# First norm's factor moved from the input to the products, its gain load moved to the end: one core of a layer with attention, scan and experts

## The chip, the cores and the metric

One NeuronCore of a Trainium2 chip runs the program. The metric is the device time of one execution in microseconds, the median of several runs. The kernel before takes 455.46 us (three runs, 455.26 to 455.54).

## What is computed

256 tokens of 1024 channels go through one layer: a norm, a projection of 5632 columns, two mixers (stick-breaking attention and a gated recurrence in chunks), gates, an output projection, a second norm, a router that gives each token 2 of 16 experts, the experts, and a last norm. What matters here is the first line of the mixer:

```python
def rmsnorm(x, g):
    var = jnp.mean(xf * xf, axis=-1, keepdims=True)
    return xf * lax.rsqrt(var + EPS) * g

h = rmsnorm(x, ln1_g)
proj = h @ w_in
```

The factor rsqrt(var + EPS) is one number for each token; g is one number for each channel. The factor can therefore be put on h or, token by token, on proj.

## The kernel before

TensorE multiplies in fp32r, and each operand is split in a high and a low part (h and l in the names): three products stand for one (hh, hl, lh). ScalarE makes the high part by a copy, VectorE or GpSimd the low part by a subtraction (`split`).

**Start.** `x2` holds x as two tiles of 128 tokens, loaded by two transfers on SyncE's queue. TensorE runs small matmuls on the identity (`warm`), and the row of gains `ln1_g` is transposed to a column `g1c`. For each of the two token tiles ScalarE squares x with a running sum, `rms_scale` forms the factor (Ln and Exp on ScalarE, one Newton step on VectorE), and VectorE multiplies x by it (`xn`). TensorE transposes `xn` in sixteen 128x128 blocks into four PSUM banks (`pts`, tags B0, B1, C0, C1), and from there ScalarE writes `hTH` and VectorE `hTL`, channel block by channel block, times `g1c`.

**Projection.** `COLS` and `WIDE` list the order of the weight columns: ten chunks of 256 columns (`half`), then six of 512 columns in two halves each (`wide`). `pre(n)` loads the weights of chunk n into a ring of three buffers, 1 MB each, and splits them. A chunk of the first ten is 48 products of 128x128 by 128x256 into one PSUM bank (tags A0 and A1 in turn), with the columns on the partitions and the tokens along the row. Chunk 0 runs its three parts one behind the other (L315); the others run hh, hl, lh for each channel block (`mm3`, L202 to L204). Behind each chunk comes its eviction: `ev_f` for chunks 0 and 1 (sigmoid, then the decay), `ev_q` for 2 and 3 (silu, then a product with kS on GpSimd), `ev_g` for 4 and 5, plain copies (qkT) for 6 to 9. `tasks` hangs the mixers' own pieces behind chunks: `vectors` (transposes of small constants) behind the first half of chunk 0, `diag` (the matmuls `pd` on GpSimd's product, then `dg` and `at`) behind chunk 4, the seven `level`s of the recurrence from chunk 5 on. A level needs masks (`lmask`) that GpSimd makes at the start.

**Order.** TensorE's instructions run as they are written. For the other engines a scheduler sets the order; `tc.issue_after(i)` puts instructions of the same engine behind i, `nosync` adds such an edge by hand.

**Experts.** Eight pairs of experts: for each, gate, up and down weights of 12 MB go through a ring of twenty buffers that the earlier stages leave (the list `state["tags"]`, tL the last of them), all on SyncE's queue, in the order of `load_gu` and `load_d`. TensorE runs the gate products, the up products, the scatter of the pair before (`py`), transposes, and the down products. `load_gain` loads `final_g`, spread over 128 partitions (0.5 MB), into tL; it stands in the last pair between the gate and the up weights:

```python
    def load_gu(p):
        for nm, w in (("g", w_gate), ("u", w_up)):
            if p == NP - 1 and nm == "u":
                load_gain()
```

Of the kernel before, what the change touches and what calls it, by code (L numbers as in the profile page):

```python
# [9 lines left out]
F32 = mybir.dt.float32  # L10
F32R = mybir.dt.float32r
# [7 lines left out]
P = 128  # L19
# [11 lines left out]
def hybrid_kernel(ctx: ExitStack, tc: tile.TileContext, x, ln1_g, w_in, w_bsb, w_bhg, hg_norm_g,  # L31
# [43 lines left out]
    act_set(EXPLN)  # L75
# [6 lines left out]
    nc.scalar.dma_start(rowa, ln1_g.rearrange("(k p) -> k p", p=P))  # L82
    nc.scalar.dma_start(rows[0:8], hg_lb.rearrange("r (k p) -> (r k) p", p=P))
# [33 lines left out]
    nc.gpsimd.memset(lmask, 1.0)  # L117
    for i, B in enumerate(LV):
        mv = lmask[:, i].rearrange("p (n b) -> p n b", b=B)
        n = 64 // B  # L120
        nc.gpsimd.affine_select(mv, mv, [[-2 * B, n], [0, B]], ALU.is_ge, 0.0, base=0,
                                channel_multiplier=1)
        nc.gpsimd.affine_select(mv, mv, [[2 * B, n], [0, B]], ALU.is_ge, 0.0, base=B - 1,
                                channel_multiplier=-1)
# [20 lines left out]
    warm(8, "A1")  # L145
# [7 lines left out]
    warm(5, "A1")  # L153

    def rms_scale(dst, ss, n, nm):
# [4 lines left out]
        nc.vector.tensor_scalar(v, ss, -0.5 / n, -0.5 * EPS, ALU.mult, ALU.add)  # L160
        act(y, y, AF.Exp, scale=-0.5)
# [20 lines left out]
    def split(raw, shape, k, pieces=1, pool=()):  # L182
# [4 lines left out]
        for i in range(pieces):  # L187
            sl = slice(i * n, i * n + n)
            if pieces == 4 and i >= 2:
                nc.vector.tensor_copy(h[:, sl], raw[:, sl])  # L190
            else:
                marks["split"] = act(h[:, sl], raw[:, sl], AF.Copy).ins
            low = (nc.gpsimd if i in pool else nc.vector).tensor_sub(l[:, sl], raw[:, sl], h[:, sl].bitcast(F32))  # L193
# [21 lines left out]
    def pre(n):  # L215
# [4 lines left out]
        elif n < NCH:  # L220
            c = COLS[n]
            raw = load(wv[:, :, c * 256:(c + 1) * 256], [KT, 256])
            chunks[n] = split(raw, [KT, 256], "p%d" % c, **({"pieces": 4, "pool": (0, 1, 3)} if n == 0 else {"pieces": 2}))
# [6 lines left out]
    marks["xn"] = marks["g1c"]  # L230
    for t in range(2):
        with tc.issue_after(marks["xn"]):
            act(xn[:, t], x2[:, t], AF.Square, accum_out=ss1[:, t:t + 1])
            rms_scale(ss1[:, t:t + 1], ss1[:, t:t + 1], D, "n1%d" % t)
            marks["xn"] = nc.vector.tensor_scalar_mul(xn[:, t], x2[:, t], ss1[:, t:t + 1]).ins
    with tc.issue_after(marks["xn"]):
        pre(0)
    pts = [ps.tile([P, 2, NTOK], F32, name="pt%d" % k2, tag=["B0", "B1", "C0", "C1"][k2]) for k2 in range(4)]
    for t in range(2):
        for k in range(KT):  # L240
            nc.tensor.transpose(pts[k // 2][:, k % 2, t * P:(t + 1) * P], xn[:, t, k * P:(k + 1) * P], ident)
    for k2 in range(4):
        for k in (2 * k2, 2 * k2 + 1):
            marks["hT"] = act(hTH[:, k], pts[k2][:, k % 2], AF.Copy, scale=g1c[:, k:k + 1]).ins
        for k in (2 * k2, 2 * k2 + 1):
            marks["hL"] = nc.vector.scalar_tensor_tensor(hTL[:, k], pts[k2][:, k % 2], g1c[:, k:k + 1],
                                                         hTH[:, k].bitcast(F32), ALU.mult, ALU.subtract).ins
# [973 lines left out]
```

## Time and profile before

| | us |
|---|---|
| median of 3 runs | 455.46 (455.26 to 455.54) |
| the profiled execution | 457.36 |
| its span, first to last instruction | 455.6 |
| TensorE busy in the span | 434.5 (95%) |
| VectorE, ScalarE, GpSimd busy | 194.3, 150.1, 102.1 |
| mean granted TensorE clock | 0.986 |
| share of TensorE in the chain that ended last | 87% |

The span lies within the execution's time; what is around it is the difference. The chain follows the last instruction back, at each step to what released it. The granted clock is a share of 2.4 GHz. Times in the rows are microseconds from the span's start unless they say ns. L12 is a line of the kernel; L60 is the helper of every ScalarE operation. PE is TensorE, PEld its weight loads, DVE VectorE, ACT ScalarE, POOL GpSimd, SP SyncE; a q behind the name is the engine's queue. Adjacent TensorE instructions overlap in the timeline, since their ends are modelled: prices are taken from a group's length by its count.

### The profile page before, as it was taken

The page shows a single profiled execution, that of the slowest core. Times are in us where ns is not written, and L with a number is a line of the kernel's source. Part 1 is how long each engine was busy: PE and PEld are TensorE (multiplying, and loading weights), DVE is VectorE, ACT ScalarE, POOL GpSimd, SP SyncE. Part 2 cuts the span into 40 slices and gives each one's busy share as a digit, 9 for nine tenths or more (in the row PEclk, how much of TensorE's full clock was granted, in tenths as well). Part 3 has the DMA queues.
Part 4 walks back from the last instruction along what each step waited for, and adds up shares of the span by engine and source line. Part 5 has one row for each costly group of instructions (what it writes and reads, how often), then busy time and mean ns, then how long its engine had stood idle before and what let it go on. Part 6 is the DMA issues. An engine that isn't in the chain of part 4 may idle for free.

```text
span 455.6 us, 6088 instructions
## 1 busy us (share of the span) xinstructions
PE 434.5 (95%) x2429; PEld 285.5 (63%) x2429; DVE 194.3 (43%) x317; ACT 150.1 (33%) x244; POOL 102.1 (22%) x119
## 2 busy tenths in 40 slices
PE   6999999999999999999999999999999999999980
PEld 5999999987887888887754336343543436343340
DVE  4959875775744845794651202121120202111032
ACT  4654326354656855362430101101020101101122
POOL 7434943877142400081200000000000000000000
PEclk8899999999999999999999999999999999999997
DMA  8755444236867899739769999999999999976942
GB/s 286 238 179 182 135 117 162 93 96 190 292 238 270 309 325 411 278 132 372 292 227 414 388 426 421 421 421 423 421 420 424 418 421 423 420 313 229 401 155 99
DMA packets 38702, 135.31 MB, mean 297 GB/s; under 512 B 2366, under 2 KB 14714, under 8 KB 26892
## 3 DMA queue, kind: packets, MB, share of 16 engines
q1 hardware_dynamic: 38480, 134.75, 77.1%
q8 instruction: 21, 0.34, 0.3%
q0 software_dynamic: 128, 0.09, 0.2%
q14 instruction: 13, 0.11, 0.1%
q10 hardware_dynamic: 60, 0.02, 0.0%
HBM read 133.80 MB, written 1.05 MB: 296 GB/s over the span
## 4 chain that ended last, share of the span: by engine, by line
PE 87%; POOL 4%; DVE 3%; issue 2%; ACT 1%; DMA 1%; SPq 0%; POOLq 0%; ACTq 0%; DVEq 0%
PE pu L995 12%; PE pg L995 12%; PE pd L1024 10%; PE pv L300 5%; PE pv L302 5%; PE pv L301 5%; PE py L1040 4%; PE pp L202 3%; PE pp L204 3%; PE pp L203 3%; PE pg L966 3%; PE pl L371 2%; PE pd L1014 2%; PE pp L315 1%; PE pb L608 1%
## 5 line engine op out<-in xcount | busy, mean ns | idle before, releaser
L193 DVE TENSOR_TENSOR lp<-wt,hp 128x1024 fp32r<-128x1024 f32 (+1 forms) x43 | 59.5, 1403 | 24.1 <-ACT hp L60 24.1
L60 ACT ACTIVATE hp<-wt 128x1024 fp32r<-128x1024 f32 (+1 forms) x44 | 44.6, 1035 | 41.6 <-PE pp L203 26.7
L995 PE MATMUL pu<-wt,xg 128*64 128x512 f32 x256 | 57.3, 593 | 0.0
L995 PE MATMUL pg<-wt,xg 128*64 128x512 f32 x256 | 56.3, 592 | 0.0
L1024 PE MATMUL pd<-wt,mf 128*64 128x512 f32 x224 | 50.4, 598 | 0.9 <-DVE mf L1005 0.7
L721 POOL TENSOR_SCALAR rb<-ss,rb 128x1 f32<-128x1 f32 x1 | 0.5, 523 | 223.3 <-ACT junk L60 223.3
L1001 DVE SCALAR_TENSOR_TENSOR mf<-pu,cwall,mf 128x512 f32<-128x512 f32 x8 | 6.0, 752 | 93.8 <-PE pu L995 93.8
L995 PEld LDWEIGHTS pu<-wt,xg 128*64 128x64 f32 x256 | 18.5, 137 | 37.0 <-issue 35.6
L202 PE MATMUL pp<-hTH,hp 128*128 128x256 f32 x144 | 41.4, 287 | 0.0
L995 PEld LDWEIGHTS pg<-wt,xg 128*64 128x64 f32 x256 | 18.3, 137 | 36.0 <-issue 35.1
L203 PE MATMUL pp<-hTL,hp 128*128 128x256 f32 x144 | 40.7, 283 | 0.0
L204 PE MATMUL pp<-hTH,lp 128*128 128x256 f32 x144 | 40.7, 283 | 0.0
L300 PE MATMUL pv<-hp,hTH 128*128 128x512 f32 x96 | 39.7, 414 | 0.0
L301 PE MATMUL pv<-lp,hTH 128*128 128x512 f32 x96 | 37.5, 391 | 0.0
L302 PE MATMUL pv<-hp,hTL 128*128 128x512 f32 x96 | 37.5, 391 | 0.0
L1024 PEld LDWEIGHTS pd<-wt,mf 128*64 128x64 f32 x224 | 14.8, 136 | 31.7 <-issue 24.0
L1031 DVE SCALAR_TENSOR_TENSOR yh<-pd,cwall,yh 128x512 fp32r<-128x512 f32 (+1 forms) x16 | 11.7, 734 | 50.8 <-ACT yh L60 50.5
L60 ACT ACTIVATE yh<-pd,cwall 128x512 fp32r<-128x512 f32 (+1 forms) x16 | 10.8, 675 | 53.5 <-PE pd L1024 38.8
L202 PEld LDWEIGHTS pp<-hTH,hp 128*128 128x128 f32 x144 | 27.6, 191 | 0.1
L203 PEld LDWEIGHTS pp<-hTL,hp 128*128 128x128 f32 x144 | 27.6, 192 | 0.0
L204 PEld LDWEIGHTS pp<-hTH,lp 128*128 128x128 f32 x144 | 27.6, 192 | 0.0
L300 PEld LDWEIGHTS pv<-hp,hTH 128*128 128x128 f32 x96 | 18.0, 188 | 5.0 <-issue 0.8
(279 smaller groups left out, 727.5 us busy)
## 6 DMA issues: line engine op xcount, KB each, us to landing
wt<-in_w_exp_gate_dram SPq DMA_DIRECT2D x32, 1024.0 KB, 15.7
wt<-in_w_exp_up_dram SPq DMA_DIRECT2D x32, 1024.0 KB, 10.7
wt<-in_w_exp_down_dram SPq DMA_DIRECT2D x28, 1024.0 KB, 13.9
wt<-in_w_in_dram SPq DMA_DIRECT2D x22, 1024.0 KB, 5.1
wt<-in_w_out_dram SPq DMA_DIRECT2D x4, 1024.0 KB, 5.0
wt<-in_w_branch_sb_dram SPq DMA_DIRECT2D x2, 1024.0 KB
wt<-in_w_branch_hg_dram SPq DMA_DIRECT2D x2, 1024.0 KB
wt<-in_w_exp_down_dram SPq DMA_DIRECT2D x4, 512.0 KB, 12.9
```

The lines of the kernel that those rows point to most:

```text
L60: i = nc.scalar.activation(out_, in_, func, **kw)
L193: low = (nc.gpsimd if i in pool else nc.vector).tensor_sub(l[:, sl], raw[:, sl], h[:, sl].bitcast(F32))
L202: nc.tensor.matmul(dst, ah, bh, start=i == 0, stop=False)
L203: nc.tensor.matmul(dst, ah, bl, start=False, stop=False)
L204: nc.tensor.matmul(dst, al, bh, start=False, stop=i == n - 1)
L300: nc.tensor.matmul(pp, hh, wh[:, k], start=kh == k == 0, stop=False)
L301: nc.tensor.matmul(pp, hh, wl[:, k], start=False, stop=False)
L302: nc.tensor.matmul(pp, hl, wh[:, k], start=False, stop=kh == 1 and k == 3)
L966: nc.tensor.matmul(pg[:, j], xx[:, t, k * P:k * P + P], Sr[:, t * 256:t * 256 + 256], start=i == 0, stop=i == 3)
L995: nc.tensor.matmul(pt[j * 64:j * 64 + 64], xg[:, k, j * 64:j * 64 + 64], wts[nm, p, j, k // 4][:, k % 4], start=k == 0, stop=k == KT - 1)
L1024: nc.tensor.matmul(pds[c][j * 64:j * 64 + 64], aT_[:, f, j * 64:j * 64 + 64], wts["d", p, j, f // 2][:, f % 2, 512 * c:512 * c + 512], sta ...
L1040: nc.tensor.matmul(total(t, c0, c1), STa[:, p % 2, t * P:t * P + P], yh[:, hl, c0:c1], start=False, stop=False, skip_group_check=True)
```

## The change

- x is loaded by column halves of both token tiles instead of by token tiles. The transfer of `ln1_g` is issued ahead of ScalarE's table load.
- TensorE transposes x itself, right behind seven warm-up matmuls instead of thirteen; `hTH` and `hTL` are formed without the factor.
- Chunk 0's weights come in four transfers and are split in quarters by an order written out by hand (`first`), and its products run in an order of 24 steps (`todo`). Chunk 1's weights come in two transfers, and its products run by halves of the channels.
- The squares are summed in halves, two on ScalarE, two on VectorE, the later ones behind chunk 0's splits. `factors` forms both tiles' factors at once and puts each, times -1, on the diagonal of a 128x128 matrix; `spread` multiplies these by a matrix of -1 in the middle of chunk 1, which gives the factor of every token on all partitions (`fac`).
- Each of the first ten chunks is multiplied by `fac` at its eviction; the wide chunks, whose tokens lie on the partitions, take the factor as a scale. `ev_f` of chunk 0 moves behind the first half of chunk 1.
- The sums of chunks 2 and 3 go to banks B0 and B1.
- `level_masks` on GpSimd moves behind chunk 0's splits.
- `load_gain` moves behind the last pair's down weights, to buffer tH; a rarely run branch takes tL for it.

```diff
-    for t in range(2):
-        nc.sync.dma_start(x2[:, t], xv[:, t])
+    for c0 in (0, 512):
+        nc.sync.dma_start(x2[:, :, c0:c0 + 512], xv[:, :, c0:c0 + 512])
...
-    warm(8, "A1")
+    warm(5, "A1")
...
+    def x_tr(k):
+        for t in range(2):
+            nc.tensor.transpose(pts[k // 2][:, k % 2, t * P:(t + 1) * P], x2[:, t, k * P:(k + 1) * P], ident)
...
-    warm(5, "A1")
+    warm(2, "A1")
+    for k in range(KT):
+        x_tr(k)
...
+        prev["dve"] = marks["g1c"]
+        sq(0, 0)
+        sq(1, 0)
+        for k in range(6):
+            gh(k)
+            if k < 2:
+                gl(k)
+            if k == 0:
+                wh(0)
+            if k == 4:
+                wh(1)
+        wl(0)
+        wl(1)
+        wh(2)
+        gh(6)
+        gh(7)
+        wh(3)
+        for k in range(2, KT):
+            gl(k)
+        marks["low"] = wl(3)
+        wl(2)
+        sq(0, 512)
+        sq(1, 512)
...
+            nc.vector.tensor_add(ss1, ssp[:, 0], ssp[:, 1])
+            for t in range(2):
+                rms_scale(ss1[:, t:t + 1], ss1[:, t:t + 1], D, "n1%d" % t)
+            for t in range(2):
+                marks["dg"] = nc.vector.tensor_scalar(xn[:, 0, t * P:t * P + P], ident, ss1[:, t:t + 1], -1.0,
+                                                      ALU.mult, ALU.mult).ins
...
+        for t in range(2):
+            nc.tensor.matmul(pf[:, t * P:t * P + P], negone, xn[:, 0, t * P:t * P + P], start=True, stop=True)
+        nc.vector.tensor_copy(fac, pf)
...
+            todo = [(0, 0), (0, 1), (1, 0), (1, 1), (0, 2), (0, 3), (1, 2), (1, 3), (2, 0), (2, 1), (0, 4), (0, 5),
+                    (1, 4), (1, 5), (2, 2), (2, 3), (0, 6), (0, 7), (1, 6), (1, 7), (2, 6), (2, 7), (2, 4), (2, 5)]
...
-        act(qs[:, sl], pp, AF.Sigmoid)
-        nc.vector.tensor_mul(qs[:, sl], qs[:, sl], pp)
+        nc.vector.tensor_mul(qk0[:, sl], pp, facb)
+        act(qs[:, sl], qk0[:, sl], AF.Sigmoid)
+        nc.vector.tensor_mul(qs[:, sl], qs[:, sl], qk0[:, sl])
...
-                        act(qkT[:, 1, sl], pp, AF.Copy)
+                        nc.vector.tensor_mul(qkT[:, 1, sl], pp, facb)
...
-            if p == NP - 1 and nm == "u":
-                load_gain()
...
-        gf["g"] = blk("tL", [2, D], name="gfin")
+        gf["g"] = blk("tH", [2, D], name="gfin")
...
         load_d(p)
+        if p == NP - 1:
+            load_gain()
```

In `first`, `gh(k)` and `gl(k)` are hTH and hTL of channel block k, `wh(i)` and `wl(i)` the high and low quarter i of the weights (`wh(0)` on VectorE, the others on ScalarE; `wl(2)` on VectorE, the others on GpSimd), and `sq(t, c0)` half the squares of token tile t (t = 1 on VectorE). In `todo` the first number is the part (hh, hl, lh), the second the channel block; each step is two products.

TensorE before, from the program's start to the second chunk (pt are the transposes, pp the products, hp and lp the weights' high and low part):

```order
L142 MATMUL warm_124<-ident 128x128 x8
L151 MATMUL pcol<-ident,rowt 128x8
L142 MATMUL warm_138<-ident 128x128 x5
L241 MATMUL pt_178<-ident,xn 128x128 x2
...
L241 MATMUL pt_181<-ident,xn 128x128 x2
L315 MATMUL pp_238<-hTH,hp_168 128x256 x16
L315 MATMUL pp_238<-hTL,hp_168 128x256 x16
L315 MATMUL pp_238<-hTH,lp_169 128x256 x16
L272 MATMUL pcol_287<-ident,rowt 128x20
```

And in the changed kernel (hfirst and lfirst are chunk 0's weights):

```order
L144 MATMUL warm_109<-ident 128x128 x5
L158 MATMUL pcol<-ident,rowt 128x8
L144 MATMUL warm_124<-ident 128x128 x2
L152 MATMUL pt_115<-ident,x_66 128x128 x4
...
L152 MATMUL pt_118<-ident,x_66 128x128 x4
L402 MATMUL pp_240<-hTH,hfirst 128x256 x4
L402 MATMUL pp_240<-hTL,hfirst 128x256 x4
...
L402 MATMUL pp_240<-hTH,lfirst 128x256 x8
L356 MATMUL pcol_289<-ident,rowt 128x20
```

The transposes read x_66, the loaded x, in place of xn, stand behind two warm-ups, and the products alternate between their parts.

VectorE before, from the eviction of chunk 2 to the diagonal (L332 is the second half of a silu, lp are splits, dg reads the diagonal's matmuls):

```order
L193 TENSOR_TENSOR lp_436<-wt_433,hp_435 128x1024
L332 TENSOR_TENSOR qs<-qs,pp_379 128x512
L193 TENSOR_TENSOR lp_436<-wt_433,hp_435 128x1024
L336 TENSOR_TENSOR QZ<-qs,kf 64x2x256 x2
L193 TENSOR_TENSOR lp_498<-wt_495,hp_497 128x1024
L332 TENSOR_TENSOR qs<-qs,pp_441 128x512
L193 TENSOR_TENSOR lp_498<-wt_495,hp_497 128x1024
L336 TENSOR_TENSOR QZ<-qs,kf 64x2x256 x2
L358 COPY dg<-pd 128x16
```

And in the changed kernel (cst holds fac; esg and qs take the products times the factor):

```order
L425 TENSOR_TENSOR esg<-pp_387,cst 128x512
L199 TENSOR_TENSOR lp_445<-wt_442,hp_444 128x1024
L427 TENSOR_TENSOR qs<-qs,esg 128x512
L199 TENSOR_TENSOR lp_445<-wt_442,hp_444 128x1024
L431 TENSOR_TENSOR QZ<-qs,kf 64x2x256 x2
L425 TENSOR_TENSOR esg<-pp_450,cst 128x512
L199 TENSOR_TENSOR lp_508<-wt_505,hp_507 128x1024
L427 TENSOR_TENSOR qs<-qs,esg 128x512
L199 TENSOR_TENSOR lp_508<-wt_505,hp_507 128x1024
L431 TENSOR_TENSOR QZ<-qs,kf 64x2x256 x2
L436 TENSOR_TENSOR qs<-pp_513,cst 128x512
L455 COPY dg<-pd 128x16
```

One pass more stands ahead of each chunk's first split, and one of chunk 4 (L436) ahead of dg.

SyncE's queue before, in the last pair:

```order
L177 DMA wt_3045<-in_w_exp_gate_dram 128x2048
L1047 DMA gfin<-in_final_g_dram 128x1024
L177 DMA wt_3049<-in_w_exp_up_dram 128x2048
```

And in the changed kernel:

```order
L1036 DMA wt_3074<-in_w_exp_down_dram 128x2x256
L1146 DMA gfin<-in_final_g_dram 128x1024
L1202 DMA out_dram<-sq 128x512
```

The gain's transfer has moved past four up loads and twelve down loads to the place ahead of the outputs.

## Rows read from the trace of the kernel before

**Rows 1.** Busy time by stretch: length, each engine's busy us, clock, DMA share, GB/s.
```profile
0.00:21.70 21.70, 17.30 (x102) 16.32 (x103) 14.64 (x35) 12.27 (x23) 14.29 (x35) 0.84 0.79 256
21.70:39.60 17.90, 17.90 (x151) 17.90 (x151) 12.21 (x24) 8.29 (x11) 7.18 (x7) 1.00 0.59 189
```

**Rows 2.** The same table by single microseconds, around the first chunk.
```profile
8.00:9.00 1.00, 0.00 (x0) 0.00 (x0) 0.96 (x3) 0.00 (x0) 0.00 (x0) 0.99 0.94 299
9.00:10.00 1.00, 0.94 (x5) 0.94 (x6) 0.82 (x5) 0.95 (x2) 0.23 (x1) 0.50 1.09 359
...
15.00:16.00 1.00, 1.00 (x7) 1.00 (x7) 1.00 (x4) 1.00 (x3) 1.00 (x2) 0.59 0.00 0
```

**Rows 3.** Chain of waits up to chunk 1: start, length, what ran.
```profile
1.26 4.77 DMA x<-in_x_dram
...
9.73 1.87 DVE xn L235
11.64 1.97 PE pt L241 x8
13.62 6.76 PE pp L315 x48
...
21.01 0.31 PE pp L202
```

**Rows 4.** Timeline, first 21 us: start, length, instruction, count, [idle before <- releaser].
```profile
1.75 3.78 PE L142 MATMUL warm<-ident 128*128 128x128 f32 x16 [1.75 <-POOL ident masks.py:199]
...
4.75 1.06 ACT L60 ACTIVATE xn<-x 128x1024 f32<-128x1024 f32 x1 [2.66 <-DMA x<-in_x_dram]
...
5.65 1.38 PE L142 MATMUL warm<-ident 128*128 128x128 f32 x10
...
9.05 1.15 ACT L60 ACTIVATE hp<-wt 128x512 fp32r<-128x512 f32 x2 [1.25 <-DMA wt<-in_w_in_dram]
...
11.51 0.86 DVE L190 CAST hp<-wt 128x512 fp32r<-128x512 f32 x2
...
12.07 3.13 POOL L193 TENSOR_TENSOR lp<-wt,hp 128x512 fp32r<-128x512 f32 x2
12.30 1.76 DVE L193 TENSOR_TENSOR lp<-wt,hp 128x512 fp32r<-128x512 f32 x1
12.37 3.03 ACT L60 ACTIVATE hTH<-pt,g1c 128x256 fp32r<-128x256 f32 x8 [2.17 <-PE pt L241]
13.27 3.28 PE L315 MATMUL pp<-hTH,hp 128*128 128x256 f32 x16
13.98 3.21 DVE L246 SCALAR_TENSOR_TENSOR hTL<-pt,g1c,hTH 128x256 fp32r<-128x256 f32 x8
...
16.38 2.08 PE L315 MATMUL pp<-hTL,hp 128*128 128x256 f32 x16
```

**Rows 5.** VectorE's group of the same form; then the timeline around the diagonal.
```profile
L332 DVE TENSOR_TENSOR qs<-qs,pp 128x512 f32<-128x512 f32 x2 | 1.4, 681 | 0.0
...
41.38 2.21 POOL L333 TENSOR_TENSOR esg<-qs,kf 128x512 f32<-128x512 f32 x1 [3.50 <-DVE qs L332]
...
44.07 1.84 PE L357 MATMUL pd<-cst,esg 128*128 128x2 f32 x16
...
57.45 2.08 PE L371 MATMUL pl<-QZ,kf 128*128 128x128 f32 x16 [1.00 <-POOL QZ L387]
```

**Rows 6.** The end: SyncE's longest single wait, busy time, timeline.
```profile
SPq L1047 <- PE pd L1024: 20.7, 1, 20.7
...
408.00:413.00 5.00, 4.83 (x28) 2.16 (x28) 1.09 (x4) 0.38 (x1) 0.00 (x0) 1.00 0.03 11
...
413.21 0.33 SPq L1047 DMA_DIRECT2D gfin<-in_final_g_dram  x1
...
416.45 7.04 PE L995 MATMUL pg<-wt,xg 128*64 128x512 f32 x32
...
423.32 8.03 PE L995 MATMUL pu<-wt,xg 128*64 128x512 f32 x32
```

More of the change, by code (lines that the diff above doesn't have):

```diff
@@ L159, in rms_scale @@
         act(y, ss, AF.Ln, bias=epst, scale=1.0 / n)
-        nc.vector.tensor_scalar(v, ss, -0.5 / n, -0.5 * EPS, ALU.mult, ALU.add)
-        act(y, y, AF.Exp, scale=-0.5)
+        marks["half"] = nc.vector.tensor_scalar(v, ss, -0.5 / n, -0.5 * EPS, ALU.mult, ALU.add).ins
+        marks["exp"] = act(y, y, AF.Exp, scale=-0.5).ins
         nc.vector.tensor_scalar(v, y, y, v, ALU.mult, ALU.mult)
@@ L188, in split @@
             sl = slice(i * n, i * n + n)
[L189 to L192, printed above, removed]
+            marks["split"] = act(h[:, sl], raw[:, sl], AF.Copy).ins
             low = (nc.gpsimd if i in pool else nc.vector).tensor_sub(l[:, sl], raw[:, sl], h[:, sl].bitcast(F32))
@@ L221, in pre @@
             c = COLS[n]
-            raw = load(wv[:, :, c * 256:(c + 1) * 256], [KT, 256])
-            chunks[n] = split(raw, [KT, 256], "p%d" % c, **({"pieces": 4, "pool": (0, 1, 3)} if n == 0 else {"pieces": 2}))
+            raw = load(wv[:, :, c * 256:(c + 1) * 256], [KT, 256], parts=2 if n == 1 else 1)
+            for k in (0, 4) if n == 1 else ():
+                nc.sync.dma_start(raw[:, k:k + 4], wv[:, k:k + 4, c * 256:(c + 1) * 256])
+            chunks[n] = split(raw, [KT, 256], "p%d" % c, pieces=2)
     hTH = blk("tH", [KT, NTOK], F32R, "hTH")
@@ L239, in hybrid_kernel @@
[L239 to L247, printed above, removed]
+    ssp = cp.tile([P, 2, 2], F32, name="ssp")
@@ new lines, in hybrid_kernel, with first, then, gh @@
+    fac = cst[:, 1344:1600]
+    def first():
+        raw = load(None, [KT, 256], parts=4)
+        c = COLS[0] * 256
+        h = blk("sh1", [KT, 256], F32R, name="hfirst")
+        l = blk("sl1", [KT, 256], F32R, name="lfirst")
+        for i in range(4):
+            nc.sync.dma_start(raw[:, 2 * i:2 * i + 2], wv[:, 2 * i:2 * i + 2, c:c + 256])
+        prev = {}
+        def then(key, i):
+            if key in prev:
+                nosync(i.ins, prev[key])
+            prev[key] = i.ins
+            return i.ins
+        def gh(k):
+            marks["hT"] = then("act", act(hTH[:, k], pts[k // 2][:, k % 2], AF.Copy, scale=g1c[:, k:k + 1]))
+        def gl(k):
+            marks["hL"] = then("dve", nc.vector.scalar_tensor_tensor(
+                hTL[:, k], pts[k // 2][:, k % 2], g1c[:, k:k + 1], hTH[:, k].bitcast(F32), ALU.mult, ALU.subtract))
+        def wh(i):
+            sl = slice(2 * i, 2 * i + 2)
+            if i < 1:
+                then("dve", nc.vector.tensor_copy(h[:, sl], raw[:, sl]))
+            else:
+                marks["split"] = then("act", act(h[:, sl], raw[:, sl], AF.Copy))
+        def wl(i):
+            sl = slice(2 * i, 2 * i + 2)
+            eng, key = (nc.vector, "dve") if i == 2 else (nc.gpsimd, "pool")
+            return then(key, eng.tensor_sub(l[:, sl], raw[:, sl], h[:, sl].bitcast(F32)))
+        def sq(t, c0):
+            y, s = x2[:, t, c0:c0 + 512], ssp[:, c0 // 512, t:t + 1]
+            if t:
+                then("dve", nc.vector.scalar_tensor_tensor(xn[:, t, c0:c0 + 512], y, 1.0, y, ALU.mult, ALU.mult,
+                                                           accum_out=s))
+            else:
+                then("act", act(xn[:, t, c0:c0 + 512], y, AF.Square, accum_out=s))
+        prev["dve"] = marks["g1c"]
[21 more added lines that the diff above has]
+        sq(1, 512)
+        marks["hT"], marks["wl"] = prev["act"], prev["dve"]
+        level_masks(marks["low"])
+        chunks[0] = h, l
+        split.n = 1
@@ new lines, in hybrid_kernel, with factors @@
+    first()
+    def factors():
+        with tc.issue_after(marks["hT"]), tc.issue_after(marks["wl"]), tc.high_priority():
+            nc.vector.tensor_add(ss1, ssp[:, 0], ssp[:, 1])
[4 more added lines that the diff above has]
+                                                      ALU.mult, ALU.mult).ins
@@ L508, in hybrid_kernel @@
         if n == 0:
-            with tc.issue_after(marks["hT"]), tc.issue_after(marks["hL"]):
+            with tc.issue_after(marks["hT"]), tc.issue_after(marks["half"]):
                 pre(1)
         else:
-            pre(n + 1)
+            with tc.issue_after(marks["exp"]), tc.issue_after(marks["dg"]):
+                pre(n + 1)
         if n == 6:
```

78 lines of the change are left out of this document (44 added, 34 removed).

## The prediction

> **What bounds the kernel now.** I read the table of busy time by stretch first. From 21.70 on TensorE is without a gap in the projections (17.90 of 17.90 us) at granted clock 1.00; before 21.70 it is busy 17.30 of 21.70 us at a mean clock of 0.84 [rows 1]. So a change that lets the projections begin earlier is worth what it takes off the first 21 us, as long as nothing later waits more. The table by single microseconds shows what the early time is made of: granted 0.99 in 8 to 9, 0.50 in 9 to 10 (the lower level, 1.2 GHz) and so on up to 15, 0.59 on average in 15 to 16, then the full level (2.4 GHz) [rows 2].
>
> The chain of waits says what set the start: x lands at 6.03, then the first norm (scalars and two passes over x on VectorE, the second ending at 11.60), the transposes, chunk 0's 48 products from 13.62 to 20.38, and chunk 1 from 21.01 [rows 3]. The timeline gives the pieces' prices: first warm-up matmuls 0.236 us each (3.78 by 16), later ones 0.138 (1.38 by 10); the first 16 products of chunk 0 at 0.205 (3.28 by 16), the next at 0.13 (2.08 by 16); hTH 0.38 a slice on ScalarE (3.03 by 8), hTL 0.40 on VectorE (3.21 by 8), a split's high quarter 0.575 (1.15 by 2) on ScalarE and 0.43 (0.86 by 2) as a cast on VectorE, a low quarter 1.57 on GpSimd (3.13 by 2) and 1.76 on VectorE [rows 4].
>
> Last, the end of the program: the queue stood 20.7 us at the gain's load for a buffer that the down products of pair 6 held; it left at 413.21, and the last up weights stand right behind it. The DMA engines were idle meanwhile (share 0.03 in 408 to 413), and the up products of pair 7 took 8.03 us where the gate products before them took 7.04 [rows 6].
>
> **The change part by part.**
>
> *Transposes of raw x, factor later.* TensorE's new order is five warm-ups (10 instructions, 2.36 us from 1.75, to 4.1), the gains' transpose (taken as 0.25), two warm-ups (0.94, to 5.3), then the sixteen transposes of x. The first column half of x should land near 4.75, where ScalarE's Square now starts [rows 4]; the second at 6.03 [rows 3]. A transpose costs 1.97 by 8 = 0.246 at granted 0.50 [rows 2, 3]; half of that, my estimate, at 1.00. The pair k=0,1 is then there between 5.8 and 6.3; I take 6.1.
>
> *Feeding chunk 0.* ScalarE: half a Square 0.6 (estimate: 1.06 for a whole one) ends by 5.4; hTH 0 to 4 run from 6.2 to 8.1, high quarter 1 to 8.7, hTH 5 to 9.1, quarter 2 to 9.65, hTH 6, 7 to 10.4, quarter 3 to 11.0. The first weights land at 9.05 [rows 4], 3.02 us behind x, so their quarters land 0.755 apart, at 6.8, 7.5, 8.3 and 9.05. The queue issues the third and fourth only when x has landed, as it does now with chunks 1 and 2; they lie behind bytes that are still to be moved, so I cost that at nothing (if that cover is gone, each is under 0.8). VectorE: half the squares (0.7), hTL 0, the cast of quarter 0 to 7.5, then hTL 1 to 7 to 10.9, paced by ScalarE, then low quarter 2 to 12.6 at the slow price of 1.76. GpSimd: low quarters 0, 1 and 3 end at 9.1, 10.7 and 12.6. Products can start at 7.6, behind the cast.
>
> *The clock in chunk 0, the uncertain term.* At 0.13 each 48 products take 6.24 us: 13.8. At 0.205 they take 9.84: 17.4. In neither is a feeder more than some 0.3 us late, since the order of the 24 pairs puts GpSimd's and VectorE's last quarters at the end. Now the clock fell about 2 us after TensorE fell idle at 7.03, was 0.50 through all sixteen transposes, and rose when products had run for 2.5 us, from 13.27 to about 15.8 (0.82 of that microsecond at 0.50 gives its 0.59) [rows 2, 4]. The change has no such idle stretch, but transposes stand between the warm-ups and the products. I take the same 2.5 us of products at the lower level: 12 products where the full one does 19 to 21, some 1.2 us lost, so chunk 0 ends at 15.0. The Trainium skill, "TensorE: Matmul & The Clock Gate", Part 4: PE-mode transpose, says that transposes don't bring the engine to its full clock; the rows agree, as 16 of them ran at 0.50 without a rise. Taken at its strictest (chunk 0 at 17.4), it would make the whole sum -3.1 us instead of the -5.5 below.
>
> *Chunk 1.* The constants' transposes keep their 0.63 us (20.38 to 21.01 [rows 3]), so chunk 1 starts at 15.6. Its order is now by halves, and two small fp32 matmuls spread the factor over all partitions: like two warm-ups, four instructions of 0.138, 0.55 us on TensorE. Its weights land in halves near 10.6 and 12.1 (1.51 us for half a chunk at the same rate); ScalarE splits them to 13.7, VectorE's second low half comes last, near 17.2, behind the norm's scalars and the two diagonals. TensorE needs it after 20 products, 15.6 + 20 x 0.13 = 18.2: no wait. The projections are then ahead by 21.0 - 15.6 - 0.55 = **4.8 us**.
>
> *Products multiplied by the factor.* Six of the ten chunks gain a pass of VectorE over 128x512 from PSUM, 0.681 us like the one that is there [rows 5]; two more take over copies of ScalarE, and in two the factor joins an operation that is there: eight passes more on VectorE. VectorE is busy 12.21 of 17.90 us in that stretch [rows 1]; it can carry this at the mean. Where it is tight is the diagonal: GpSimd's product of chunk 3 runs 41.38 to 43.59 and TensorE reads it at about 44, slack 0.4; dg follows, and the levels behind it already make TensorE wait 1.00 before 57.45 [rows 5]. The order puts the new pass ahead of chunk 3's split on VectorE, where it fits into the wait for ScalarE except for the 0.68 of chunk 2 that pushes it, and one more (sgt) ahead of dg. Followed through, the product comes about 0.6 late against 0.4 of slack, and dg 0.25. I charge **+0.3**; bounds 0 (the slack covers all) and 1.4 (two passes, nothing covered). The level masks move behind GpSimd's splits; their first reader is the first level, behind the diagonal of 44.07, some 30 us later: nothing. The vv copies become scalings of the same size, and the gates' evictions take the factor as their scale: nothing.
>
> *The gain last of all.* The four up loads then wait only for their own buffers, which by the round of twenty were read last by pair 5's down products, before the queue came to stand (413.21 - 20.7 = 392.5). So the 5 us of idle DMA close and the 0.99 us that TensorE waited go [rows 6]. The gain lands behind the last down weights; these now land at least 5 us earlier, and the gain is read only when the last pair's first scatter is done, so nothing waits for it. **-1.0**; bounds 0 and -1.5 (the gain's 0.5 MB out of the way, at the 3.02 us of a whole MB).
>
> Sum: -4.8 + 0.3 - 1.0 = -5.5. The profiled run took 457.36, 455.6 of it span and 1.76 around it, which the change leaves alone: 451.9. The median of the runs lies 1.90 below the profiled one, at 455.46, so the forecast is **450.0 us**.
>
> **The rivals.**
> - *Clock at the lower level through all of chunk 0* (transposes hold it down, feeders' gaps too): chunk 0 ends at 17.4, 2.4 later: 452.4. For it: 16 transposes at 0.50. Against: 3.3 us of warm-ups just before, and dense products. 22%. It is the case to which the Trainium skill's page named above points.
> - *Clock never falls*: chunk 0 ends at 13.8, 1.2 sooner, of which chunk 1's low half takes 0.4 back: 449.2. For it: TensorE is nowhere idle as it was from 7.03 to 9.06. 18%.
> - *The end gives nothing* (the up weights stay late because the engines, not the buffer, limit them): 451.0. Against: share 0.03 for 5 us. 6%.
> - *VectorE becomes the bound*: its eight added passes find no idle time, and each puts off the low half that TensorE needs next: 8 x 0.681 = 5.4 against the 0.3 charged, 455.1, no difference that shows (a measurement of this kernel tells about 0.2%, 0.9 us, from no change). Against: 5.7 us free in 17.9 [rows 1]. 2%.
> - *Slower: the clock stays low into the chunks behind.* If TensorE waits in chunk 0 and 1 for splits that come late, the lower level can last through chunks 1 and 2, 48 products each at 0.205 instead of 0.13: 2.4 + 2 x 3.6 = 9.6 more, 459.6. It decides in the second further chunk: one alone gives 450.0 + 2.4 + 3.6 = 456.0, still within those 0.9. For it: the clock was low for nearly 7 us once it had fallen [rows 2]. Against: it rose within 2.5 us of products fed just as unevenly, one per 0.205. 4%.
> - *Not what it says*: the order shows the transposes reading x, the factor behind the products and the gain last; it is left with the rest.
>
> **How the numbers follow.** Forecast 47%, rivals 22, 18, 6, 2 and 4%, and 1% for what I don't see. The low end is a clock that never falls, 449.2, with nothing charged at the diagonal (-0.3) and 0.5 more at the end: 448.4. The high end is a low clock, 452.4, with the full 1.4 at the diagonal (+1.1): 453.5. Outside lie the last two rivals, and combinations beyond these. Faster by over 0.2%: 0.94; within: 0.02; slower: 0.04.
>
> **What would show it.** In the new profile: chunk 0's products start near 7.6 and end near 15.0; chunk 1 starts near 15.6; a stretch of granted 0.50 for 2 to 4 us inside chunk 0; TensorE's wait at the second level 1.0 to 1.5; the up products of pair 7 in 7.04; no idle DMA before them. The forecast is wrong if the clock is at 0.50 up to 17 or longer, if TensorE shows waits for VectorE's low halves in chunks 1 to 5, or if chunk 1 starts later than 18.

## The result, and the profile after

The changed kernel takes **453.0 us**, the median of six runs (452.62 to 453.42). Beside it the kernel before took 455.6 (455.26 to 457.15). The medians lie 2.6 us apart; the ratio on record, which goes by all runs, is 0.9932, with a 95% interval of 0.9915 to 0.9948: faster by 0.7%, or 3.1 us (2.4 to 3.9). The forecast was 450.0, with a range of 448.4 to 453.5 and 0.94 for faster. Direction and range held; the point was 3.0 us too low, and about half of the gain that it promised is missing.

The profiled execution of the change took 453.42, with a span of 451.7. The same places in three profiled executions (the third kernel, `port`, is the kernel before with one edit; it is told of below), in us from the span's start:

| | before | port | change | change - before | change - port |
|---|---|---|---|---|---|
| chunk 1 begins | 20.94 | 19.48 | 14.91 | -6.03 | -4.57 |
| first level | 48.73 | 47.27 | 43.89 | -4.84 | -3.38 |
| second level | 57.45 | 55.99 | 52.01 | -5.44 | -3.98 |
| second sums `pm` before the gates | 146.08 | 144.62 | 140.69 | -5.39 | -3.93 |
| first products `pb` behind the gates | 174.35 | 172.89 | 170.32 | -4.03 | -2.57 |
| pair 7's gate products | 416.45 | 414.99 | 412.40 | -4.05 | -2.59 |
| scatter behind pair 7's up products | 431.28 | 429.86 | 426.23 | -5.05 | -3.63 |
| VectorE's last operation | 448.47 | 447.05 | 443.42 | -5.05 | -3.63 |
| end of the span | 455.6 | 454.3 | 451.7 | -3.9 | -2.6 |

The start of the change, TensorE's timeline (start, length, instruction, count, [idle before <- releaser]):

```profile
1.75 2.50 PE L144 MATMUL warm<-ident 128*128 128x128 f32 x10 [1.75 <-POOL ident masks.py:199]
...
5.40 2.02 PE L152 MATMUL pt<-ident,x 128*128 128x128 f32 x16
7.61 0.71 PE L402 MATMUL pp<-hTH,hfirst 128*128 128x256 f32 x4 [0.20 <-DVE hfirst L268]
...
9.30 0.74 PE L402 MATMUL pp<-hTH,hfirst 128*128 128x256 f32 x4 [0.50 <-ACT hfirst L60]
...
13.23 1.12 PE L402 MATMUL pp<-hTH,lfirst 128*128 128x256 f32 x8
...
14.91 0.75 PE L410 MATMUL pp<-hTH,hp 128*128 128x256 f32 x4
...
18.05 0.74 PE L410 MATMUL pp<-hTH,lp 128*128 128x256 f32 x4 [0.49 <-DVE lp L199]
18.63 0.61 PE L327 MATMUL pf<-xn,cst 128*128 128x128 f32 x4
```

Sixteen transposes take 2.02 us, 0.126 each, where eight took 1.97 before [rows 3]; in another profile of the same start they take 3.25, as told below. The products of chunk 0 start at 7.61 and end near 14.3. The table by stretch (length, busy us of TensorE, its weight loads, VectorE, ScalarE, GpSimd, then clock, DMA share, GB/s) answers to [rows 1, 2]:

```profile
0.00:21.70 21.70, 18.76 (x134) 17.75 (x135) 15.77 (x47) 13.06 (x26) 15.42 (x32) 1.00 0.85 278
21.70:39.60 17.90, 17.90 (x153) 17.90 (x151) 16.84 (x25) 9.00 (x12) 11.17 (x12) 1.00 0.63 203
```

The table has the granted clock at 1.00 over all of the start, where it was 0.84 on average. The trace's first clock record, at 1.00, stands at 5.61 (5.58 in the kernel before). Ahead of it there is no record and the table prints 1.00; the warm-ups ran there 0.213 apart, the transposes behind it 0.11. From 5.61 to 442.5 the clock did not fall. VectorE is busy 16.84 of 17.90 us in the second stretch, up from 12.21: near the bound, and still not one wait of TensorE there.

TensorE's waits in the change, by cause (waited for: us in total, times, longest):

```profile
PE pv L384 <- ACT gsb L60: 1.2, 1, 1.2
PE py L588 <- DVE ysb L592: 1.0, 1, 1.0
...
PE pp L402 <- ACT hfirst L60: 0.5, 1, 0.5
PE pp L410 <- DVE lp L199: 0.5, 1, 0.5
PE pl L468 <- POOL QZ L484: 0.4, 1, 0.4
```

The wait at the second level is 0.4 instead of 1.00 [rows 5]; the first line is new. It lies in the gates. What happened there, from the timeline of the change:

```profile
140.16 0.69 DVE L532 SCALAR_TENSOR_TENSOR nt<-pm,nt 128x512 f32<-128x512 f32 x1 [3.60 <-ACT nt L60]
...
141.32 0.69 DVE L533 SCALAR_TENSOR_TENSOR osb<-nt,osb 128x512 f32<-128x512 f32 x1 [0.46 <-DVE nt L532]
...
141.97 1.23 DVE L199 TENSOR_TENSOR lp<-wt,hp 128x1024 fp32r<-128x1024 f32 x1
142.15 2.20 POOL L534 TENSOR_TENSOR osb<-osb 128x512 f32<-128x512 f32 x1 [4.69 <-DVE osb L533]
...
144.43 2.15 POOL L535 TENSOR_TENSOR osb<-osb,esg 128x512 f32<-128x512 f32 x1
...
146.61 0.63 ACT L60 ACTIVATE yhgyha<-osb 128x512 fp32r<-128x512 f32 x1 [2.63 <-POOL osb L535]
147.15 0.61 ACT L60 ACTIVATE nt<-osb 128x512 f32<-128x512 f32 x1
...
147.67 0.67 ACT L60 ACTIVATE gsb<-pv,ss 128x512 f32<-128x512 f32 x1
...
148.39 0.50 PE L384 MATMUL pv<-hp,hTH 128*128 128x512 f32 x1 [1.20 <-ACT gsb L60]
```

The same operations of VectorE and GpSimd in the kernel before:

```profile
146.35 0.69 DVE L436 SCALAR_TENSOR_TENSOR osb<-nt,osb 128x512 f32<-128x512 f32 x1
...
147.19 1.30 POOL L437 TENSOR_TENSOR osb<-osb 128x512 f32<-128x512 f32 x1 [4.43 <-DVE osb L436]
147.37 4.43 DVE L193 TENSOR_TENSOR lp<-wt,hp 128x1024 fp32r<-128x1024 f32 x2 [0.32 <-ACT hp L60]
```

Read it backwards. TensorE waits for a bank that ScalarE empties (`gsb`). ScalarE stands in line behind `yhgyha`, which waits for GpSimd's second product; that is late because GpSimd's first product took 2.20 us, where it took 1.30 in the kernel before. It began 0.18 behind VectorE's split `lp`, and that split could begin first because `osb` on VectorE came 0.46 after `nt`, an operation of VectorE itself; by then the high part that the split reads was there, which in the kernel before it still waited for.

The end, which answers to [rows 6]:

```profile
419.27 7.04 PE L1094 MATMUL pu<-wt,xg 128*64 128x512 f32 x32
...
422.01 0.38 SPq L1146 DMA_DIRECT2D gfin<-in_final_g_dram  x1
...
426.23 2.12 PE L1139 MATMUL py<-yh,mr 128*128 128x512 f32 x8
...
444.17 1.69 SPq L1202 DMA_DIRECT2D out_dram<-sq  x1
445.95 0.39 SPq L1204 DMA_DIRECT2D out_dram<-sq  x1
```

The up products take 7.04 as forecast. The third output store took 1.69 us to issue, and the span ends 8.3 us behind the start of VectorE's last operation, against 7.1 in the profile of before. In the eleven further profiles below this distance is 7.25 to 8.1. One of the last two stores always takes 1.1 to 1.5 us to issue there, in four profiles the third and in seven the fourth, with the gain early and late. With the gain early the distance is 7.1 to 7.5 in four profiles, with the gain late 7.4 to 8.3 in nine. I take most of it for scatter of single executions; whether the late gain adds a few tenths stays open.

### The profile page after: what moved, and what is told of

Same layout as the page of the kernel before. It is cut to its first block, busy times and chain, and to the rows that moved or that the text cites. A ratio compares the mean times of both kernels' runs of the same rounds, so it can differ in the third digit from the quotient of the medians.

```text
span 451.7 us, 6090 instructions
## 1 busy us (share of the span) xinstructions
PE 430.3 (95%) x2421; PEld 282.0 (62%) x2421; DVE 199.6 (44%) x330; ACT 150.1 (33%) x243; POOL 105.9 (23%) x119
## 4 chain that ended last, share of the span: by engine, by line
PE 50%; DVE 2%; POOL 1%; issue 1%; ACT 1%; POOLq 0%; ACTq 0%; DVEq 0%
PE pu L1094 12%; PE pg L1094 12%; PE pd L1123 10%; PE py L1139 4%; PE pg L1065 3%; PE pd L1113 2%; PE pq L892 1%; PE pq L893 1%; PE pq L891 1%; PE pg L875 1%; PE pT L1103 1%; DVE mf L1104 1%; POOL lo L199 1%; PE plg L771 1%; PE py L940 1%
## 5 line engine op out<-in xcount | busy, mean ns | idle before, releaser
L199 DVE TENSOR_TENSOR lp<-wt,hp 128x1024 fp32r<-128x1024 f32 x42 | 56.8, 1370 | 15.9 <-ACT hp L60 15.7
L1094 PE MATMUL pu<-wt,xg 128*64 128x512 f32 x256 | 56.3, 592 | 0.0
L60 ACT ACTIVATE hp<-wt 128x1024 fp32r<-128x1024 f32 x42 | 43.3, 1052 | 34.7 <-issue 17.1
L208 PE MATMUL pp<-hTH,hp 128*128 128x256 f32 x128 | 36.8, 287 | 0.0
L209 PE MATMUL pp<-hTL,hp 128*128 128x256 f32 x128 | 36.2, 283 | 0.0
L210 PE MATMUL pp<-hTH,lp 128*128 128x256 f32 x128 | 36.2, 283 | 0.0
L208 PEld LDWEIGHTS pp<-hTH,hp 128*128 128x128 f32 x128 | 24.5, 191 | 0.1
L209 PEld LDWEIGHTS pp<-hTL,hp 128*128 128x128 f32 x128 | 24.5, 192 | 0.0
L210 PEld LDWEIGHTS pp<-hTH,lp 128*128 128x128 f32 x128 | 24.5, 192 | 0.0
## 6 DMA issues: line engine op xcount, KB each, us to landing
wt<-in_w_exp_down_dram SPq DMA_DIRECT2D x4, 512.0 KB, 17.6
```

The lines of the kernel that those rows point to most:

```text
L60: i = nc.scalar.activation(out_, in_, func, **kw)
L208: nc.tensor.matmul(dst, ah, bh, start=i == 0, stop=False)
L209: nc.tensor.matmul(dst, ah, bl, start=False, stop=False)
L210: nc.tensor.matmul(dst, al, bh, start=False, stop=i == n - 1)
L1094: nc.tensor.matmul(pt[j * 64:j * 64 + 64], xg[:, k, j * 64:j * 64 + 64], wts[nm, p, j, k // 4][:, k % 4], start=k == 0, stop=k == KT - 1)
```

## The experiments

All ratios are against the kernel before, run beside each, and go by all runs. Differences from the change are between medians that were taken at different times.

**The end alone, and the start alone.** `tail_only` is the kernel before with the gain (the last norm's `final_g`) loaded last; `start_only` is the change without it.

```diff
-            if p == NP - 1 and nm == "u":
-                load_gain()
...
         load_d(p)
+        if p == NP - 1:
+            load_gain()
```

> The kernel before with one part of the change: the gain is loaded last of all. If the up weights of pair 7 were late only because they stood behind the gain, its up products take 7.0 us instead of 8.0 and the time falls by 1.0 us, to about 454.6. If the output stores give the time back at the end, as the trace of the change suggests (they land 1.1 us later against the last operation on VectorE), the fall is 0 with the up products at 7.0 all the same.

> The change without the gain loaded last. If the end is worth 1.0 us and adds to the start, this takes 454.0, with pair 7's up products at 8.0 us. If the output stores are slow whatever stands ahead of them, the time from VectorE's last operation to the end of the span is the same as in the change, about 7.5 us; if the early gain had kept them fast, it is 6.4 us, as before the change, and the whole takes 453.0, no more than the change.

`tail_only`: 455.47 against 456.12, ratio 0.9981 (0.9966 to 0.9996), so -0.9 us (-0.2 to -1.6), with pair 7's up products at 7.04. `start_only`: 453.89, ratio 0.9949 (0.9929 to 0.9968), 0.9 us above the change, with the up products at 8.08 and the distance to the end 7.5. The end is worth 0.9 by both ways, near the 1.0 of the forecast, and the intervals leave room for a few tenths that the stores may take back.

`tail_only` showed something else. Its start is that of the kernel before, yet chunk 1 began at 19.33, 1.6 us earlier than in the profile of before.

**Why the start of before differs.** Two guesses were tried: the clock, by filling TensorE's idle time, and two engines that meet.

```diff
-    warm(5, "A1")
+    warm(12, "A1")
```

> The kernel before with seven more warm-up matmuls (14 instructions, 1.9 us) in TensorE's idle stretch from 7.03 to 9.06. If idleness dropped the clock, it stays at 1.00 up to chunk 0, whose transposes and products then run at the higher level: chunk 1 begins up to 3.4 us earlier (products 0.205 against 0.13 over the first 2.5 us, transposes 0.246 against 0.126 each), less what the norm holds back, so some 1.2 to 2 us off the time. If the transposes drop the clock by themselves, nothing changes: 455.6. If the runs of the kernel before differ because their clock falls in some and not in others, these runs lie closer together.

456.8, ratio 1.0006 (0.999 to 1.0022): no gain. The clock was indeed held up longer: it is 1.00 up to 11, through the first eight transposes.

```profile
10.00:11.00 1.00, 0.22 (x2) 0.00 (x0) 1.00 (x1) 0.20 (x1) 1.00 (x2) 1.00 1.10 356
11.00:12.00 1.00, 0.37 (x2) 0.37 (x3) 1.00 (x3) 0.00 (x0) 1.00 (x3) 0.83 1.10 352
12.00:13.00 1.00, 1.00 (x7) 1.00 (x6) 1.00 (x3) 0.64 (x2) 1.00 (x2) 0.50 1.10 349
```

TensorE then had nothing to do (busy 0.22 and 0.37), since the norm's second pass took 1.78 us, and the lower level came at 11.65 all the same. The twelve runs fall into two groups, four at 455.4 to 455.5 and eight at 456.7 to 457.8.

```diff
-{"pieces": 4, "pool": (0, 1, 3)}
+{"pieces": 4, "pool": (1, 2, 3)}
```

> The kernel before with GpSimd's first low quarter of chunk 0 given to VectorE behind the norm, and VectorE's to GpSimd. In the profile of before the second pass of the norm took 1.86 us beside that operation of GpSimd and chunk 1 began at 20.9; where the end alone was changed it took 0.75, GpSimd's 1.81, and chunk 1 began at 19.3. If the two engines' meeting there, which falls out one way or the other from run to run, makes the runs of before differ (455.1 to 458.4), the pass takes 0.75 here, chunk 1 begins at 19.4 and all runs lie at 455.0 to 456.3. If the spread has another cause, it stays, and the median stays at that of before.

All twelve runs lie between 455.35 and 456.38, where the kernel before, run beside it, went from 455.1 to 458.83, seven of its 19 runs above 456.6. The medians agree (455.91 and 455.71; ratio 0.9987, 0.9968 to 1.0006). In its timeline:

```profile
9.74 0.75 DVE L235 TENSOR_SCALAR xn<-x,ss 128x1024 f32<-128x1024 f32 x1
10.18 1.44 POOL L193 TENSOR_TENSOR lp<-wt,hp 128x512 fp32r<-128x512 f32 x1 [2.42 <-ACT hp L60]
```

The pass takes 0.75 and chunk 1 begins at 19.48, as expected. In `tail_only`, where the pass won the meeting, GpSimd paid:

```profile
9.62 0.75 DVE L235 TENSOR_SCALAR xn<-x,ss 128x1024 f32<-128x1024 f32 x1
9.68 1.81 POOL L193 TENSOR_TENSOR lp<-wt,hp 128x512 fp32r<-128x512 f32 x1 [1.94 <-ACT hp L60]
```

In the profile of before it was the pass that paid:

```profile
9.73 1.86 DVE L235 TENSOR_SCALAR xn<-x,ss 128x1024 f32<-128x1024 f32 x1
9.77 1.27 POOL L193 TENSOR_TENSOR lp<-wt,hp 128x512 fp32r<-128x512 f32 x1 [2.02 <-ACT hp L60]
```

So the profiled run of before, 1.9 above its median, was one in which the pass lost, and the forecast had read its gain off that run. Three of the 19 runs lie at 458.6 to 458.8, some 2.9 above the median; the 1.5 us of the lost pass doesn't reach that, and no trace shows what else they lost. The Trainium skill, "SBUF — State Buffer", section "Who interferes with whom", says that an operation of VectorE which takes a second pair of ports shares that pair with GpSimd, that the operation issued first keeps it to its end, and that the other stands still. The lengths agree: the loser takes 0.5 to 1.1 us longer. The recorded starts don't tell the winner when they are this close: the pass is recorded first in both profiles, by 0.04 where it lost and by 0.06 where it won.

**The clock in the change.** One warm-up instead of seven.

```diff
-    warm(5, "A1")
+    warm(1, "A1")
...
-    warm(2, "A1")
```

> The change with one warm-up matmul instead of seven. If warm-ups are what lets the transposes of x run at 0.126 us each, these take 0.25 each, 4 us in all, and the first products 0.205 each until 2.5 us of them have run: chunk 1 begins 1 to 3 us later than at 14.9, and the time is 454 to 456. If the warm-ups do nothing, the transposes begin with the landing of x at 4.5 instead of 5.4 and the time falls by up to 0.5 us, to 452.5.

452.8, ratio 0.9928 (0.9902 to 0.9953): no loss, and no gain that shows. The transposes and products in its timeline:

```profile
4.75 3.67 PE L152 MATMUL pt<-ident,x 128*128 128x128 f32 x16 [2.01 <-DMA x<-in_x_dram]
8.08 0.86 PE L401 MATMUL pp<-hTH,hfirst 128*128 128x256 f32 x4
8.78 0.64 PE L401 MATMUL pp<-hTL,hfirst 128*128 128x256 f32 x4
...
14.77 0.74 PE L409 MATMUL pp<-hTH,hp 128*128 128x256 f32 x4
```

The transposes run 0.21 apart to the last, where the change's took 0.126 each. The second product comes 0.34 behind the first, the others 0.12 apart, the full rate; the trace's first clock record, at 1.00, stands at 8.38. Chunk 1 begins 10.0 us behind the landing of x (4.73), against 10.5 in the change (4.42). So the slow transposes cost nothing that shows.

The warm-ups alone don't make the transposes fast either. On TensorE seven profiles are alike up to there (the change, `start_only`, `gates`, `pad`, `nofac`, `lpfirst`, `twobanks`), and their first clock record stands anywhere from 5.24 to 8.13. At about that time the transposes go from 0.213 to 0.11 apart: all sixteen take 2.02 us in the change and 3.25 in `start_only`. In none does the clock fall again before 440.

The Trainium skill, "TensorE: Matmul & The Clock Gate", Part 4: PE-mode transpose, says that transposes don't bring the engine to its full clock. `cold` can't settle that, since the first product had begun 0.3 us before the clock's record. `tail_only` differs from it:

```profile
8.95 3.41 PE L241 MATMUL pt<-ident,xn 128*128 128x128 f32 x16 [2.08 <-DVE v_n L160]
...
10.00:11.00 1.00, 1.00 (x7) 1.00 (x6) 1.00 (x2) 0.11 (x1) 1.00 (x1) 0.50 1.10 347
11.00:12.00 1.00, 1.00 (x7) 1.00 (x6) 1.00 (x2) 0.62 (x2) 1.00 (x3) 0.53 1.11 350
12.00:13.00 1.00, 1.00 (x10) 0.92 (x9) 1.00 (x3) 1.00 (x4) 1.00 (x2) 1.00 1.10 349
```

The clock was at 0.50 from 8.54 and rose at 11.95, when TensorE had done nothing but transposes since 8.95; its first product began at 12.11. In `port` the clock rose at 12.33 and the first product began at 12.36. So here transposes didn't hold the clock down: it came up while nothing else ran.

**The passes and the banks.** `nofac` leaves out the multiplications at the evictions of the first ten chunks, `twobanks` puts chunks 2 and 3 back.

```diff
-        nc.vector.tensor_mul(fE[:, sl], pp, facb)
-        act(fE[:, sl], fE[:, sl], AF.Sigmoid)
+        act(fE[:, sl], pp, AF.Sigmoid)
...
-tag="%s%d" % ("B" if n in (2, 3) else "A", n % 2)
+tag="A%d" % (n % 2)
```

> The change without the multiplication by the factor at the evictions of the first ten chunks (the output lacks it there). Forecast in the prediction: the eight passes of VectorE cost 0.3 us, so 452.7, with TensorE's wait at the second level near 0.2. If VectorE hides them all, 453.0. If they also push VectorE's split into GpSimd's products at the gates, the wait of 1.20 us at 148.4 goes with them, 451.6.

> The change with the sums of chunks 2 and 3 in the banks of chunks 0 and 1 again; the orders are the same. The prediction costed the banks at nothing. In the change VectorE's products with the factor that empty the two banks ended near 21.8 and 22.8, and chunks 2 and 3 begin near 21.9 and 27.6. If TensorE waits only for the first, the time stays within 0.2 of 453.0. If the evictions end later than the trace suggests, chunk 2 begins up to 0.5 us later, 453.5, which is then what the two further banks are worth.

`nofac`: 452.03, ratio 0.9908 (0.9878 to 0.9937), 1.0 below the change. But two waits changed in opposite ways: the one at the gates is gone, and the one at the second level is back at its old size:

```profile
52.67 2.08 PE L465 MATMUL pl<-QZ,kf 128*128 128x128 f32 x16 [1.00 <-POOL QZ L481]
```

So the passes don't lengthen that wait; with them it is 0.6 shorter. The rows show where. Before, and then in the change:

```profile
46.20 5.78 POOL L360 TENSOR_TENSOR at<-ident,dg 128x1024 f32<-128x1024 f32 x2 [2.61 <-DVE dg L358]
47.30 0.87 DVE L342 SCALAR_TENSOR_TENSOR esg<-pp,cols,esg 128x256 f32<-128x256 f32 x2
...
41.37 4.84 POOL L457 TENSOR_TENSOR at<-ident,dg 128x1024 f32<-128x1024 f32 x2 [2.36 <-DVE dg L455]
42.34 4.16 DVE L439 SCALAR_TENSOR_TENSOR esg<-qs,cols,esg 128x256 f32<-128x256 f32 x2
```

With the pass, VectorE's `esg` reads `qs` instead of the bank; it takes 4.16 for two instead of 0.87, and GpSimd's `at` beside it takes 0.94 less (in `nofac` 5.77 again). GpSimd's next two operations give 0.34 of it back, which leaves the 0.6. It is a third meeting of the two engines, which the change turned in its favour. `twobanks`: 452.82, ratio 0.9931 (0.9915 to 0.9947), the same as the change: the two further banks are worth nothing here.

**The wait at the gates.** First by its consequence: ScalarE's copy of the bank goes ahead of the operation that waits for GpSimd.

```diff
+                    if (n, m) == (17, 0):
+                        marks["gate"] = ev
...
-        act(yhg[0][:, s], o, AF.Copy)
+        with tc.issue_after(marks["gate"]):
+            act(yhg[0][:, s], o, AF.Copy)
```

> The change with ScalarE's order altered at one place: the copy of the first gate's sums out of their bank stands ahead of the operation that waits for GpSimd. If TensorE's wait of 1.20 us at 148.4 is only a bank that comes free late, it goes, and the time falls by 1.2 us, to about 451.8. If GpSimd's late product is what matters, the wait moves to the gates' products that read it and the time stays at 453.0.

451.56, ratio 0.9898 (0.9876 to 0.992): 1.4 below the change, and TensorE's wait is gone although GpSimd's product still takes 2.20. It was only the bank. Then by its cause, the pause of VectorE:

```diff
+    nc.vector.memset(cp.tile([P, 1], F32, name="spare"), 0.0)
```

> The change with one more operation on VectorE, a memset of 128x1 near 2 us that nothing reads; all orders are else the same. In the change, and in three kernels made from it, VectorE paused 0.46 us between two of its own operations at the gates (141.3), its split then began 0.2 us ahead of GpSimd's product instead of behind it, the product took 2.20 us instead of 1.30, and TensorE waited 1.20; with the second low half moved far ahead of it the pause was not there. If the pause hangs on the place of the operations in VectorE's stream, one operation more takes it away: wait gone, product 1.30, time 451.8. If it hangs on what the engines do at that time, all stays: wait 1.20, 453.0.

451.75, ratio 0.9901 (0.9884 to 0.9919), with nothing done but one memset more:

```profile
141.39 0.69 DVE L533 SCALAR_TENSOR_TENSOR nt<-pm,nt 128x512 f32<-128x512 f32 x1 [3.60 <-ACT nt L60]
...
142.18 0.69 DVE L534 SCALAR_TENSOR_TENSOR osb<-nt,osb 128x512 f32<-128x512 f32 x1
...
143.02 1.30 POOL L535 TENSOR_TENSOR osb<-osb 128x512 f32<-128x512 f32 x1 [4.33 <-DVE osb L534]
...
143.20 4.43 DVE L200 TENSOR_TENSOR lp<-wt,hp 128x1024 fp32r<-128x1024 f32 x2 [0.32 <-ACT hp L60]
```

`osb` follows `nt` without the pause, GpSimd begins 0.18 ahead of the split instead of behind it, its product takes 1.30 and the split pays (4.43 for two), which nobody waits for. (This execution is the slowest of its five, 452.70, by a wait of 1.4 us in chunk 1, far ahead of the gates; from the second `pm` to `pb` it takes 28.39 against 29.63.) The rest of the wait's story is therefore shown. That the pause goes with the operation's place in VectorE's stream, the records bear out. All five kernels with the change's own stream there (`start_only`, `gates`, `cold`, `twobanks` and the change) have it at this spot, and `nofac`, with fewer operations ahead of it, has 0.46 at the next pair of the same operations. Counted with the semaphore instructions, the operation behind the pause is the 192nd of VectorE's records in all six. In `pad`, `lpfirst` and `best` it is the 193rd, the 192nd is the semaphore instruction that waits for `nt`, and there is no pause. What makes the pause stays open. It also means that `nofac` lost the gates' wait in this way, not by its lighter VectorE: against `pad` (451.75), which has all the passes, it is no faster.

**The wait in chunk 1.** The second low half goes ahead of the norm's last scalars and the diagonals.

```diff
-                rms_scale(ss1[:, t:t + 1], ss1[:, t:t + 1], D, "n1%d" % t)
...
+    def newton():
+        with tc.issue_after(marks["low"]), tc.high_priority():
...
                 pre(1)
+            newton()
```

> The change with the second low half of chunk 1 ahead of the norm's last scalars and the two diagonals on VectorE. If TensorE's wait of 0.49 us at 18.05 is their doing, it goes, and as the factor's spreading is ready some 0.1 us late in its place the time falls by 0.3 to 0.5 us, to 452.6. If the wait only moves to the spreading of the factor, or to the levels further on, it stays at 453.0.

451.31, ratio 0.9884 (0.9851 to 0.9917), more than expected. The pause at the gates is gone here too, which brings 1.3 (from the second `pm` to `pb` 28.37 against 29.63). From the start of chunk 1 to the first product of the diagonal it takes 23.58 us (15.71 to 39.29) where the change takes 24.32, and the wait of 0.49 is gone. But chunk 1 began 0.8 later in this execution, so at the first level nothing is left of that (43.95 against 43.89). Part of the delay is one more meeting: at the end of chunk 0 VectorE's low quarter began 0.08 ahead of GpSimd's and took 0.68 instead of 1.80, GpSimd's took 1.76 instead of 1.30, and TensorE waited 0.18 for it. By the medians 0.4 is left for the wait in chunk 1, which is not shown. That wait itself differs between kernels that are alike up to it: 0.3 in `start_only`, `gates`, `nofac` and `twobanks`, and 1.4 in `pad`, where the second half of the weights came 1.5 us later than in the change.

**Together.**

> The change with three edits together: the gate's sums copied out ahead of the operation that waits for GpSimd, the second low half of chunk 1 ahead of the norm's last scalars, and one warm-up matmul instead of seven. The first two each took the wait at the gates away, so their gains share those 1.2 us: 0.4 of chunk 1 and 0.2 of the warm-ups come on top of 451.6, about 451.0. If the early start without warm-ups, whose transposes took 0.24 us each, only moves the wait to the weights, 451.3.

450.96, ratio 0.9893 (0.9872 to 0.9914): faster than before by 1.1% and than the change by 2.0 us, as expected for the sum. Its interval overlaps those of `gates`, `pad` and `lpfirst`, so it isn't shown to beat these. What it has from `gates` is that ScalarE's order, not the accident of the pause, keeps TensorE from waiting.

## Why the prediction was right and wrong

- **Start, -4.8: right by the trace it was read from, by other terms.** Chunk 1 began at 14.91, not 15.6, because the rival that the clock never falls, at 18%, came true: once up, it stayed at 1.00. TensorE had no idle stretch between the warm-ups and the products, as the forecast had it; it was the 2.5 us at the lower level, charged at 1.2, that did not come. Against that, chunk 1's second low half was ready at 18.0, not 17.2, as the second half of its weights came at 13.75, not 12.1; TensorE stood before it at 17.6, not 18.2: a wait of 0.49 where the text said "no wait", and one that it names as a sign of being wrong. The shift up to the first level is -4.84; that it comes so near to -4.8 is luck, two errors against each other. The reason given for the first rival, that transposes hold the clock down, is refuted by `tail_only` and `port`. What the parts of the start are worth (the factor behind the products, the loads in halves and quarters, the order by hand) no run separates: only the start as a whole is shown.
- **Diagonal, +0.3: wrong in sign.** The wait at the second level fell from 1.00 to 0.40, and `nofac` shows that it is the passes that changed it. The forecast followed the added passes to GpSimd's product of chunk 3, but not to the meeting behind it, where VectorE's `esg` now stands beside GpSimd's `at` (4.84 instead of 5.78). That VectorE could carry them was right (no wait in 17.9 us, 1.06 us free).
- **The gates, no term: missed.** The wide chunks' evictions were put at "nothing"; each takes the factor as its scale, 0.68 instead of 0.59 on average, and that was indeed nothing. But behind them 1.4 us went into a wait whose elements all existed before: ScalarE's fixed order, GpSimd's product, the split beside it. Only the margin, some 0.2 us between two starts, tipped over. No row of before shows the pause, so it could not be priced; that the copy of a bank stood behind an operation that waits for GpSimd could be seen.
- **The gain last, -1.0: right.** Up products 7.04, DMA share 1.01 from 404 to 409, the stretch that answers to the idle one, and -0.9 by two kernels. The rival by which the end gives nothing is out, as are VectorE as the bound and the clock low into later chunks.
- **From the trace to the median: the step that failed.** The text took the trace's 5.5 off the median, as if the 1.90 between that run and the median were the same in both kernels. They were not: 1.46 of them are the norm's pass losing its meeting with GpSimd, just at the place that the change rebuilds. Against `port`, whose runs don't differ in that, the same terms give -4.57 for chunk 1's start and -3.63 for the last operation.

So the 3.0 us missed are two halves: within the profiles the change gave 3.9 instead of 5.5 (1.4 lost at the gates, 1.1 in the stores of that one execution, 0.9 gained at the level), and the profiled run of before stood 1.9 above its median where that of the change stood 0.4 above. That 453.0 lies within the range all the same is luck: its upper end stood for a low clock and a full charge at the diagonal, and neither came.

## What to carry to other kernels

Before a gain is taken off a median, ask what made the profiled run differ from the median run: if it lies in the stretch that the change replaces, it is no gain. Where VectorE and GpSimd meet with starts 0.2 us apart on a path that something waits for, any edit can turn the meeting over; price it at both outcomes, and look at what stands in line behind the slower one. And when an edit seems to cost something far from where it was made, try a kernel with one operation that does nothing before believing in the reason: here it was worth 1.2 us.

## What the hardware showed that I had not expected

- A pause of 0.46 us on VectorE between two of its own operations, in all six kernels that show it ahead of the 192nd of its recorded instructions, which one further 128x1 memset 139 us earlier takes away.
- The clock rose while TensorE did nothing but transposes (`tail_only` at 11.95, `port` at 12.33).
- The column of the granted clock reads 1.00 where the trace has no clock record yet: `cold`'s sixteen transposes run 0.21 apart from 4.75 on, with 1.00 in each of those microseconds, and its first record stands at 8.38. At the start the time of one instruction tells the rate, not that column.
- Of the last two output stores one takes 1.1 to 1.7 us to issue, the other 0.3 to 0.7, and which one it is changes from run to run.
